# Expert routing set by VectorE's time, bfloat16 look-ups, and scattered weights laid out token by token

## The chip, the core and the metric

The kernel runs on one core of one Trainium2 chip. Five engines work side by side, each through a queue of its own in order: PE (TensorE, matrix products into PSUM), DVE (VectorE), ACT (ScalarE), POOL (GpSimd) and SP, which issues the loads. The metric is the device time in microseconds (us), the median of three runs: 2158.25 us (2157.36 to 2162.6).

## The reference

256 tokens of width 1024 pass through two blocks. What matters here is the PEER layer, which occurs twice in the second block. Its core:

```
q = (t @ w_q).reshape(n_tok, 8, 2, 128)                 # 8 heads, two halves
sc = einsum("thpd,hpnd->thpn", q, subkeys)              # 128 scores per half
sv, si = top_k(sc, 16)                                  # 16 best of each half
cand = sv[:, :, 0, :, None] + sv[:, :, 1, None, :]      # 256 sums per head
cidx = si[:, :, 0, :, None] * 128 + si[:, :, 1, None, :]
top_v, pos = top_k(cand, 16)
idx = take_along_axis(cidx, pos); g = softmax(top_v)    # 128 experts per token
h = einsum("cd,ced->ce", t, u_tab[idx])
a = g * gelu(h)
out = einsum("ce,ced->cd", a, v_tab[idx])
```

There are 16384 experts, each with a row of `u_tab` and of `v_tab`.

## The kernel before

The kernel gathers nothing. It multiplies all 256 tokens by all 128 tiles of `u_tab` (128 experts each; loop `for i in range(P)`, L1132), keeps the gelu of every product in `X` (`xa` for tiles below XA = 100, `xb` for the rest), and multiplies it by a weight that is zero for all experts that a token did not choose. Then `X` is multiplied by `v_tab` (L1178 onward).

**One step i of the loop.** `dense_t` (L136) fetches a 512 KB tile (one of four `raw` buffers), `split_now` (L109) makes it into a high part (`hi`, a cast on ACT, L121) and a low part (`lo`, a subtraction on DVE or POOL, L122), each with three buffers (HL), and PE runs 24 products of 256 columns into one of two PSUM banks (L132 to L134). ACT applies gelu (L1150, or L1146 followed by a product on DVE, L1147, once weights are there). For i below J1 + 2 = 42 the subtraction is on POOL, afterwards on DVE.

**Routing (i below J1 = 40).** It runs beside these steps, mostly on DVE, as a list of 36 jobs (L1118 to L1125) spread evenly by their count over the 40 steps. For each half `a` of the tokens: `candidates` and `best` find the 16 best of each head; `ranks` turns positions into two ranks; `weights` makes the softmax, with an Exp on ACT (L1064) between DVE's subtraction (L1062) and its sum (L1066); `keys` looks up the index behind each rank by comparing with 0 to 15 (L1050), multiplying with the list (L1055) and summing (L1057), in four calls of 64 ranks by 16 entries; `turn` transposes both keys and the weights on PE (L1078) and copies them, the keys with ACT (L1081), the weights with DVE (L1084). Two more functions, Exp and Gelu, each want a table on ACT, so each Exp between two gelus brings two table loads.

**Scatter (i from 40 to 123).** 64 times, for four tokens each, `scatter` compares both keys with 0 to 127 (`o`, L1092), multiplies by the weight in two parts (`wi`, L1099), and PE forms the four tokens' weights for all experts, eight products of 128 columns of float16 into one bank `G` (L1106). The bank is laid out token by token, each with 128 experts side by side. DVE multiplies the part for tiles already done into `X` (L1113), ACT copies the rest there (L1116); in `X` neighbouring experts of one token lie 1 KB apart.

**Order.** The Tile framework orders each engine's queue ahead of the run by the program order, its priorities and a modelled time. `split` has a priority 200 instructions ahead. `tc.issue_after(x)` puts those instructions of a block that run on x's engine behind x in that queue; it waits for nothing.

Of the kernel before, what the change touches and what calls it, by code (L numbers as in the profile page):

```python
# [10 lines left out]
F32 = mybir.dt.float32  # L11
F32R = mybir.dt.float32r
BF16 = mybir.dt.bfloat16
# [37 lines left out]
def two_blocks(ctx: ExitStack, tc: tile.TileContext, io, out):  # L51
# [37 lines left out]


    count, relief, fetched, pin, pinned = [0], [0], [0], [None], [0]

    more = []

# [14 lines left out]
    def split_now(raw, pool_share, into):  # L109
        count[0] += 1  # L110
        hi, lo = into or [stream.tile([P, D], F32R, tag=t, name=t, bufs=HL) for t in ("hi", "lo")]
        on_pool = pool_share and count[0] % pool_share == 0
        if relief[0] > 0 and into is None:
            relief[0] -= 1
            on_pool = True
        if pinned[0] > 0 and into is None:
            pinned[0] -= 1
            with tc.issue_after(pin[0]):
                S.copy(out=hi, in_=raw)
        else:  # L120
            S.copy(out=hi, in_=raw)  # L121
        (G if on_pool else V).tensor_tensor(out=lo, in0=raw, in1=hi.bitcast(F32), op=OP.subtract)  # L122
        return hi, lo

    def in_order(dst, src):
# [798 lines left out]
    def peer(l, entered, nxt):  # L924
        acts, nat = (xh, xl), entered.nat
        with ExitStack() as es:
            with ExitStack() as es1:
# [52 lines left out]
                for a in range(2):  # L980
# [4 lines left out]
                flat = X[1][:, 16:22].rearrange("p n g t -> p n (g t)")  # L985
# [3 lines left out]
                e = X[1][:, 20:22].rearrange("p n g t -> p (n g t)").bitcast(BF16).rearrange(  # L989
                    "p (n k) -> p n k", k=16)  # L990
                for n in range(12):
                    if n:
# [29 lines left out]
                def ranks(a):  # L1022
                    pos = state["pos"].rearrange("p h k -> p (h k)")
                    tmp = [one.tile([P, P], U32, tag=f"t{i}", name=f"t{i}") for i in range(4)]
                    V.tensor_scalar(tmp[0], pos, 4, None, op0=OP.logical_shift_right)
                    V.tensor_scalar(tmp[1], pos, 2, None, op0=OP.logical_shift_right)
                    V.tensor_scalar(tmp[2], pos, 15, None, op0=OP.bitwise_and)
                    V.tensor_scalar(tmp[3], pos, 3, None, op0=OP.bitwise_and)
                    m = one.tile([P, P], F32, tag="m_", name="m_")
                    V.tensor_scalar(m, pos, 64.0, None, op0=OP.is_ge)  # L1030
                    ra = one.tile([P, P], F32, tag="ra", name="ra")
                    rb = one.tile([P, P], F32, tag="rb", name="rb")
                    V.scalar_tensor_tensor(out=ra, in0=tmp[1], scalar=12.0, in1=tmp[0],
                                           op0=OP.subtract, op1=OP.subtract)
# [4 lines left out]
                    V.tensor_tensor(out=rb, in0=rb, in1=tmp[2], op=OP.add)  # L1039
                    state["rank"] = (ra, rb)  # L1040
# [5 lines left out]
                def keys(a, side, part):  # L1046

                    hs = slice(part * 4, part * 4 + 4)
                    cs = slice(part * 64, part * 64 + 64)
                    V.tensor_tensor(  # L1050
                        out=e, in0=state["rank"][side][:, cs].unsqueeze(2).to_broadcast([P, 64, 16]),
                        in1=iota_f[:, 0:16].unsqueeze(1).to_broadcast([P, 64, 16]), op=OP.is_equal)
                    lists = state["sif"].rearrange("q (h p) k -> q h p k", p=2)[:, hs, side]
                    e4 = e.rearrange("q (h k) a -> q h k a", h=4)
                    V.tensor_tensor(out=e4, in0=e4, in1=lists.unsqueeze(2).to_broadcast([P, 4, 16, 16]),  # L1055
                                    op=OP.mult)
                    V.tensor_reduce(out=state["key"][side][:, cs], in_=e, axis=AX.X, op=OP.add)  # L1057

                def weights(a):
                    tv = state["tv"]  # L1060
                    g = one.tile([P, 8, 16], F32, tag="g", name="g")
                    V.tensor_tensor(out=g, in0=tv, in1=tv[:, :, 0:1].to_broadcast([P, 8, 16]),  # L1062
                                    op=OP.subtract)
                    S.activation(out=g, in_=g, func=AF.Exp)  # L1064
# [6 lines left out]
                    state["g"] = g  # L1071

                def turn(a):
                    s = slice(a * P, (a + 1) * P)
# [12 lines left out]
                def scatter(tg, done):  # L1087
# [10 lines left out]
                    for i in range(2):  # L1098
# [1 line left out]
                            out=wi[i].rearrange("p n (b c) -> p n b c", c=4),  # L1100
                            in0=o[:, 0:4].rearrange("p n (b c) -> p n b c", c=4),
                            in1=gt[i][:, s].unsqueeze(2).to_broadcast([P, 4, 32, 4]), op=OP.mult)
                    ps = bank(p_tr, "G").rearrange("p (t i) -> p t i", t=4)
                    for t in range(4):
                        for i in range(2):
                            PE.matmul(out=ps[:, t], lhsT=o[:, 4 + t], rhs=wi[i][:, t],  # L1106
                                      start=i == 0, stop=i == 1)
                    for i0, xt in ((0, X[0]), (XA, X[1])):
                        n = xt.shape[1]
                        dst = xt[:, :, tg].rearrange("p i t -> p t i")  # L1110
                        old = min(max(done - i0, 0), n)
                        if old:
                            V.tensor_tensor(out=dst[:, :, :old], in0=ps[:, :, i0:i0 + old],  # L1113
                                            in1=dst[:, :, :old], op=OP.mult)
                        if old < n:
                            S.copy(out=dst[:, :, old:], in_=ps[:, :, i0 + old:i0 + n])  # L1116

                jobs = [lambda n=n: (subkeys(n), lists(n)) for n in range(12, 16)]  # L1118
                for a in range(2):
                    for part in range(2):  # L1120
                        jobs.append(lambda a=a, part=part: candidates(a, part))
                        jobs += [lambda a=a, h=h: best(a, h) for h in range(4 * part, 4 * part + 4)]
                    jobs.append(lambda a=a: (ranks(a), weights(a)))
                    jobs += [lambda a=a, s=s, p=p: keys(a, s, p) for s in range(2) for p in range(2)]
                    jobs.append(lambda a=a: turn(a))  # L1125
                at = {}
                for i, job in enumerate(jobs):
                    at.setdefault(i * J1 // len(jobs), []).append(job)
                for tg in range(64):
                    at.setdefault(J1 + tg * (J2 - J1) // 64, []).append(tg)  # L1130
                ready = 0
                for i in range(P):  # L1132
# [2 lines left out]
                        two = es1.enter_context(sbuf("gw2", 2, "right"))  # L1135
                    for job in at.get(i, []):
                        if callable(job):
                            job()
                        else:
                            scatter(job, i)  # L1140
                            ready = job + 1
                    ps = dense_t(io["peer_u"][l, i], acts, int(i < J1 + 2)).rearrange(
                        "p (g t) -> p g t", t=4)
                    if ready:
                        h = two.tile([P, 64, 4], F32, tag="h", name="h")
# [1 line left out]
                        V.tensor_tensor(out=xs(i)[:, :ready], in0=xs(i)[:, :ready], in1=h[:, :ready],  # L1147
                                        op=OP.mult)
                    if ready < 64:
                        S.activation(out=xs(i)[:, ready:], in_=ps[:, ready:], func=AF.Gelu)  # L1150
            acc = accumulators()
            late = []

# [194 lines left out]
```

## Time and profile before

| | |
|---|---|
| median of three runs | 2158.25 us |
| the profiled execution: time, span | 2159.3 us, 2157.5 us |
| PE busy | 2100.2 us (97%) |
| DVE busy | 1571.3 us (73%) |
| ACT busy | 1097.2 us (51%) |
| POOL busy | 348.9 us (16%) |
| mean granted TensorE clock | 0.988 of full speed |

The first PEER layer's steps i begin at about 443 us of the span and its scatter at about 568 us; the second layer's at about 1383 and 1507 us. In the rows further down, an idle time in brackets stands for the time before that instruction, with what ended it.

### The profile page before, as it was taken

What the parts mean: (1) busy time and instruction counts of PE and PEld (TensorE: products, weight loads), DVE (VectorE), ACT (ScalarE), POOL (GpSimd) and SP (SyncE); (2) the same over time, 40 slices, a digit from 0 to 9 for tenths busy, and PEclk for the clock granted to TensorE, in tenths of its full rate; (3) what the DMA queues carried; (4) which work ended last, traced back from release to release, by engine and by line L of the source; (5) the groups of instructions that cost most, each with busy time, mean ns of one, the idle gap of its engine ahead of it and who ended that gap; (6) DMA issues with size and microseconds to landing.
All of it is one profiled execution on the core that took longest, in us unless ns stands there. A gap on an engine that the chain in (4) does not pass through costs nothing. (4 is left out here: it accounts for less than half of the span.)

```text
span 2157.5 us, 37694 instructions
## 1 busy us (share of the span) xinstructions
PE 2100.2 (97%) x14288; PEld 1907.1 (88%) x14288; DVE 1571.3 (73%) x3045; ACT 1097.2 (51%) x1979; POOL 348.9 (16%) x167
## 2 busy tenths in 40 slices
PE   8999999998999999999999999989999999999998
PEld 7899989998999999888888777989999998888886
DVE  4456778699488998566566685995889996566565
ACT  4556545344555444555555574444554445555554
POOL 3210011278500000000000232588000000000000
PEclk9999999999999999999999999999999999999999
DMA  6634737345555455666666551545555456666664
GB/s 238 218 125 154 256 119 234 99 147 156 180 163 163 153 160 172 189 193 194 189 195 200 206 197 57 169 147 162 164 165 158 158 162 198 189 192 193 189 194 137
DMA packets 104437, 373.94 MB, mean 173 GB/s; under 512 B 12096, under 2 KB 14144, under 8 KB 103744
## 3 DMA queue, kind: packets, MB, share of 16 engines
q1 hardware_dynamic: 103968, 371.01, 54.8%
q8 instruction: 112, 1.84, 0.3%
q14 instruction: 69, 0.57, 0.1%
q10 hardware_dynamic: 288, 0.52, 0.1%
HBM read 370.44 MB, written 1.05 MB: 172 GB/s over the span
## 5 line engine op out<-in xcount | busy, mean ns | idle before, releaser
L132 PE MATMUL mm<-xh,hi 128*128 128x256 f32 x2880 | 834.9, 290 | 23.8 <-ACT xa L1150 22.2
L134 PE MATMUL mm<-xh,lo 128*128 128x256 f32 x2880 | 817.5, 284 | 0.4 <-POOL lo L122 0.4
L133 PE MATMUL mm<-xl,hi 128*128 128x256 f32 x2880 | 817.6, 284 | 0.0
L121 ACT CAST hi<-raw 128x1024 fp32r<-128x1024 f32 x600 | 632.5, 1054 | 283.6 <-issue 145.9
L122 DVE TENSOR_TENSOR lo<-raw,hi 128x1024 fp32r<-128x1024 f32 x484 | 592.2, 1223 | 248.1 <-ACT hi L121 244.0
L132 PEld LDWEIGHTS mm<-xh,hi 128*128 128x128 f32 x2880 | 555.1, 193 | 28.7 <-ACT xa L1150 23.7
L133 PEld LDWEIGHTS mm<-xl,hi 128*128 128x128 f32 x2880 | 555.6, 193 | 0.3
L134 PEld LDWEIGHTS mm<-xh,lo 128*128 128x128 f32 x2880 | 554.9, 193 | 1.0 <-POOL lo L122 0.8
L122 POOL TENSOR_TENSOR lo<-raw,hi 128x1024 fp32r<-128x1024 f32 x118 | 304.2, 2588 | 251.0 <-ACT hi L121 241.4
L1174 PE MATMUL acc<-hi,al 128*128 128x512 f32 x976 | 304.1, 393 | 0.0
L1174 PE MATMUL acc<-lo,ah 128*128 128x512 f32 x976 | 302.4, 391 | 0.0
L1174 PE MATMUL acc<-hi,ah 128*128 128x512 f32 x976 | 301.5, 390 | 0.0
L1174 PEld LDWEIGHTS acc<-hi,ah 128*128 128x128 f32 x976 | 183.1, 188 | 41.8
L1174 PEld LDWEIGHTS acc<-hi,al 128*128 128x128 f32 x976 | 183.4, 188 | 39.7
L1174 PEld LDWEIGHTS acc<-lo,ah 128*128 128x128 f32 x976 | 183.3, 188 | 38.7
L1163 ACT CAST ah<-xa 128x256 fp32r<-128x256 f32 x200 | 81.2, 407 | 241.5 <-PE acc L1174 241.5
L1164 DVE TENSOR_TENSOR al<-xa,ah 128x256 fp32r<-128x256 f32 x200 | 85.0, 426 | 99.2 <-PE acc L1174 99.2
L294 POOL TENSOR_TENSOR enl<-raw,enh 128x1024 fp32r<-128x1024 f32 x5 | 12.4, 2488 | 823.0 <-ACT enh L293 823.0
L1116 ACT COPY xa<-G 128x240 f32<-128x240 f32 (+22 forms) x92 | 35.1, 382 | 180.0 <-DVE xa L1113 139.0
L1113 DVE TENSOR_TENSOR xa<-G,xa 128x400 f32<-128x400 f32 (+31 forms) x128 | 111.4, 870 | 0.0
L1099 DVE TENSOR_TENSOR wi<-o,gt 128x512 f16<-128x512 f16 x256 | 106.5, 456 | 1.0
L1092 DVE TENSOR_TENSOR o<-iota_k,ij 128x1024 f16<-128x1024 f16 x128 | 94.6, 741 | 11.9 <-PE G L1106 10.7
(461 smaller groups left out, 2113.4 us busy)
## 6 DMA issues: line engine op xcount, KB each, us to landing
raw<-in_peer_u_dram SPq DMA_DIRECT2D x256, 512.0 KB, 3.6
raw<-in_peer_v_dram SPq DMA_DIRECT2D x256, 512.0 KB, 4.2
raw<-in_peer_w_q_dram SPq DMA_DIRECT2D x24, 512.0 KB, 3.8
raw<-in_conv_w_in_dram SPq DMA_DIRECT2D x20, 512.0 KB, 3.9
raw<-in_w_rest_dram SPq DMA_DIRECT2D x18, 512.0 KB, 3.8
raw<-in_w_qk_dram SPq DMA_DIRECT2D x16, 512.0 KB, 4.5
more<-in_w_rest_dram SPq DMA_DIRECT2D x10, 512.0 KB, 3.7
raw<-in_w_v_dram SPq DMA_DIRECT2D x8, 512.0 KB, 4.6
```

What stands on the lines that cost most here:

```text
L121: S.copy(out=hi, in_=raw)
L122: (G if on_pool else V).tensor_tensor(out=lo, in0=raw, in1=hi.bitcast(F32), op=OP.subtract)
L132: PE.matmul(out=ps, lhsT=ah, rhs=bh, start=first and i == 0, stop=False)
L133: PE.matmul(out=ps, lhsT=ah, rhs=bl, start=False, stop=False)
L134: PE.matmul(out=ps, lhsT=al, rhs=bh, start=False, stop=last and i == n - 1)
L1092: V.tensor_tensor(out=o.rearrange("p n (b c) -> p n b c", c=4), in0=iota_k.rearrange("p (b c) -> p b c", c=4).unsqueeze(1).to_broadcast(fo ...
L1099: V.tensor_tensor(out=wi[i].rearrange("p n (b c) -> p n b c", c=4), in0=o[:, 0:4].rearrange("p n (b c) -> p n b c", c=4), in1=gt[i][:, s]. ...
L1113: V.tensor_tensor(out=dst[:, :, :old], in0=ps[:, :, i0:i0 + old], in1=dst[:, :, :old], op=OP.mult)
L1116: S.copy(out=dst[:, :, old:], in_=ps[:, :, i0 + old:i0 + n])
L1163: S.copy(out=act[0], in_=src)
L1164: V.tensor_tensor(out=act[1], in0=src, in1=act[0].bitcast(F32), op=OP.subtract)
L1174: PE.matmul(out=acc[a][half], lhsT=p[:, s], rhs=r[:, half * 512:(half + 1) * 512], start=i == 0 and w == 0, stop=i == P - 1 and w == 2)
```

## The change

- **Jobs** carry a cost and a flag; they are placed by the sum of the costs (28 units) over JOBS = 35 steps instead of by count over 40. `weights` loses its first and second instruction to two jobs: `shifted` (the subtraction, together with `ranks`) and `exponentials` (the Exp, behind the last gelu in ACT's queue), which follow in the order `shifted` + `ranks`, two `keys`, `exponentials`, `weights`. `turn` comes TURN = 4 steps after `weights`.
- **Splits in the routing stage** are on POOL in steps of flagged jobs (lists, candidates, best), on DVE in steps of the others and from step 36 on.
- **Each job** is traced within `issue_after` the last split that ran on DVE.
- **Look-ups** take 128 ranks at once. The ranks are written four times over in bfloat16, the lists are bfloat16, and the sum is four additions of halves instead of a reduction. The two keys have two buffers each. The scratch `e` has twice the size.
- **`turn`** copies the keys with DVE.
- **`scatter`** lays the bank `G` out expert by expert with the four tokens side by side: PE's 128 output columns lie 16 bytes apart, and DVE and ACT read the bank straight and write runs of four tokens (16 bytes).

```
-J1, J2, LATE, XA = 40, 124, 6, 100
+JOBS, TURN, J1, J2, LATE, XA = 35, 4, 40, 124, 6, 100
...
+        low = (G if on_pool else V).tensor_tensor(out=lo, in0=raw, in1=hi.bitcast(F32),
+                                                  op=OP.subtract)
+        if not on_pool:
+            last_split[0] = low.ins
...
+                    rank = [one.tile([P, P, 4], BF16, tag=f"rank{i}", name=f"rank{i}")
+                            for i in range(2)]
...
-                    V.tensor_tensor(out=ra, in0=ra, in1=tmp[0], op=OP.add)
+                    V.tensor_tensor(out=rank[0], in0=four(ra), in1=four(tmp[0]), op=OP.add)
...
-                    state["key"] = [one.tile([P, P], F32, tag=f"key{i}", name=f"key{i}")
+                    state["key"] = [two.tile([P, P], F32, tag=f"key{i}", name=f"key{i}")
                                     for i in range(2)]
-                    state["sif"] = one.tile([P, 16, 16], F32, tag="sif", name="sif")
+                    state["sif"] = one.tile([P, 16, 16], BF16, tag="sif", name="sif")
...
+                def keys(a, side):
+
                     V.tensor_tensor(
+                        out=e.rearrange("q n (b c) -> q n b c", c=4),
+                        in0=state["rank"][side].unsqueeze(2).to_broadcast([P, P, 4, 4]),
+                        in1=iota_f[:, 0:16].rearrange("q (b c) -> q b c", c=4).unsqueeze(1)
+                        .to_broadcast([P, P, 4, 4]), op=OP.is_equal)
+                    lists = state["sif"].rearrange("q (h p) k -> q h p k", p=2)[:, :, side]
+                    e4 = e.rearrange("q (h k) a -> q h k a", h=8)
+                    V.tensor_tensor(out=e4, in0=e4, in1=lists.unsqueeze(2).to_broadcast([P, 8, 16, 16]),
                                     op=OP.mult)
-                    V.tensor_reduce(out=state["key"][side][:, cs], in_=e, axis=AX.X, op=OP.add)
+                    for n in (8, 4, 2):
+                        V.tensor_tensor(out=e[:, :, 0:n], in0=e[:, :, 0:n], in1=e[:, :, n:2 * n],
+                                        op=OP.add)
+                    V.tensor_tensor(out=state["key"][side], in0=e[:, :, 0], in1=e[:, :, 1], op=OP.add)
...
+                def exponentials():
+                    with tc.issue_after(state["gelu"]):
+                        S.activation(out=state["g"], in_=state["g"], func=AF.Exp)
...
-                        S.copy(out=ij[:, 32 * a:32 * a + 32, c],
+                        V.tensor_copy(out=ij[:, 32 * a:32 * a + 32, c],
...
-                    ps = bank(p_tr, "G").rearrange("p (t i) -> p t i", t=4)
+                    ps = bank(p_tr, "G").rearrange("p (t i) -> p i t", t=4)
...
-                            PE.matmul(out=ps[:, t], lhsT=o[:, 4 + t], rhs=wi[i][:, t],
+                            PE.matmul(out=ps[:, :, t], lhsT=o[:, 4 + t], rhs=wi[i][:, t],
...
-                            V.tensor_tensor(out=dst[:, :, :old], in0=ps[:, :, i0:i0 + old],
+                            V.tensor_tensor(out=dst[:, :old], in0=ps[:, i0:i0 + old],
...
+                jobs = [(1.1, True, lambda n=n: (subkeys(n), lists(n))) for n in range(12, 16)]
                 for a in range(2):
                     for part in range(2):
+                        jobs.append((0.3, True, lambda a=a, part=part: candidates(a, part)))
+                        jobs += [(0.5, True, lambda a=a, h=h: best(a, h))
+                                 for h in range(4 * part, 4 * part + 4)]
+                    jobs.append((2.0, False, lambda a=a: (shifted(a), ranks(a))))
+                    jobs += [(2.1, False, lambda a=a, s=s: keys(a, s)) for s in range(2)]
+                    jobs.append((0.2, False, exponentials))
+                    jobs.append((0.8, False, weights))
...
-                            job()
+                            with tc.issue_after(last_split[0]):
+                                job()
...
-                    ps = dense_t(io["peer_u"][l, i], acts, int(i < J1 + 2)).rearrange(
+                    ps = dense_t(io["peer_u"][l, i], acts, int(i < len(by_pool) and by_pool[i])).rearrange(
```

## Rows read from the trace of the kernel before

**Rows 1.** PE's timeline: start, duration, instruction, idle time before and its releaser.

```profile
468.30 0.58 PE L132 MATMUL mm<-xh,hi 128*128 128x256 f32 x1 [3.27 <-ACT xa L1150]
...
520.60 0.58 PE L132 MATMUL mm<-xh,hi 128*128 128x256 f32 x1 [5.65 <-ACT xa L1150]
...
1404.27 0.39 PE L132 MATMUL mm<-xh,hi 128*128 128x256 f32 x1 [3.27 <-ACT xa L1150]
...
1458.23 0.58 PE L132 MATMUL mm<-xh,hi 128*128 128x256 f32 x1 [9.20 <-ACT xa L1150]
```

**Rows 2.** ACT's timeline, three of the four Exps.

```profile
465.31 0.31 ACT L1064 ACTIVATE g<-g 128x128 f32<-128x128 f32 x1 [3.44 <-DVE g L1062]
...
517.61 0.31 ACT L1064 ACTIVATE g<-g 128x128 f32<-128x128 f32 x1 [5.18 <-DVE g L1062]
...
1455.23 0.31 ACT L1064 ACTIVATE g<-g 128x128 f32<-128x128 f32 x1 [8.74 <-DVE g L1062]
```

**Rows 3.** Windows: length, busy time by engine, PEclk, DMA share, GB/s.

```profile
474.00:476.00 2.00, 2.00 (x18) 2.00 (x17) 2.00 (x5) 0.99 (x2) 1.21 (x1) 0.89 0.66 246
...
524.00:526.00 2.00, 2.00 (x12) 2.00 (x12) 2.00 (x5) 0.10 (x1) 0.60 (x1) 0.59 0.36 57
...
1404.00:1406.00 2.00, 1.73 (x14) 1.73 (x15) 2.00 (x1) 1.44 (x3) 2.00 (x2) 1.00 0.00 0
...
1464.00:1466.00 2.00, 2.00 (x17) 2.00 (x17) 1.97 (x4) 0.91 (x2) 1.29 (x1) 0.93 0.51 197
```

**Rows 4.** Windows of the first layer: routing, early scatter, late scatter (PE, PEld, DVE, ACT, POOL).

```profile
460.00:545.00 85.00, 76.08 (x590) 75.53 (x590) 84.19 (x164) 38.99 (x58) 67.14 (x25) 0.92 0.49 150
580.00:740.00 160.00, 160.00 (x1477) 158.35 (x1476) 139.38 (x246) 84.11 (x224) 0.00 (x0) 1.00 0.52 162
740.00:840.00 100.00, 99.00 (x904) 96.96 (x903) 97.15 (x166) 43.66 (x119) 0.00 (x0) 1.00 0.51 159
```

**Rows 5.** DVE by form, 400 to 562 us: busy us, mean ns, idle before.

```profile
L1055 DVE TENSOR_TENSOR xb<-xb,sif 128x1024 bf16<-128x1024 bf16 x8 | 21.7, 2710 | 0.1
L1057 DVE TENSOR_REDUCE key<-xb 128x64 f32<-128x1024 bf16 x8 | 9.6, 1206 | 0.1
...
L1050 DVE TENSOR_TENSOR xb<-ra,iota_f 128x1024 bf16<-128x1024 f32 x4 | 8.3, 2083 | 0.0
L1050 DVE TENSOR_TENSOR xb<-rb,iota_f 128x1024 bf16<-128x1024 f32 x4 | 7.3, 1830 | 0.0
...
L1099 DVE TENSOR_TENSOR wi<-o,gt 128x512 f16<-128x512 f16 x2 | 5.2, 2626 | 0.0
L122 DVE TENSOR_TENSOR lo<-raw,hi 128x1024 fp32r<-128x1024 f32 x4 | 4.8, 1205 | 0.0
```

**Rows 6.** DVE by form, 560 to 845 us, where POOL is idle from 580 us.

```profile
L1099 DVE TENSOR_TENSOR wi<-o,gt 128x512 f16<-128x512 f16 x126 | 48.1, 423 | 0.5
L1092 DVE TENSOR_TENSOR o<-iota_k,ij 128x1024 f16<-128x1024 f16 x62 | 42.9, 691 | 6.0 <-PE G L1106 5.4
L1113 DVE TENSOR_TENSOR xa<-G,xa 128x400 f32<-128x400 f32 x18 | 19.7, 1092 | 0.0
...
L1147 DVE TENSOR_TENSOR xb<-xb,h 128x244 f32<-128x244 f32 x2 | 0.8, 424 | 0.0
...
L1113 DVE TENSOR_TENSOR xa<-G,xa 128x244 f32<-128x244 f32 x1 | 0.7, 710 | 0.0
```

**Rows 7.** DVE's timeline, its wait at the end of routing.

```profile
568.53 0.69 DVE L1084 CAST gt<-tr 128x512 f16<-128x512 f32 x1 [23.93 <-ACT ij L1081]
```

**Rows 8.** PE's timeline, one scatter's products and the step behind them.

```profile
1510.26 0.62 PE L1106 MATMUL G<-wi,o 128*128 128x128 f16 x8
1510.69 0.36 PE L132 MATMUL mm<-xh,hi 128*128 128x256 f32 x1
1510.89 0.28 PE L133 MATMUL mm<-xl,hi 128*128 128x256 f32 x1
1511.01 0.28 PE L134 MATMUL mm<-xh,lo 128*128 128x256 f32 x1
```

More of the change, by code (lines that the diff above doesn't have):

```diff
@@ L91, in two_blocks @@
     count, relief, fetched, pin, pinned = [0], [0], [0], [None], [0]
+    last_split = [None]
     more = []
@@ L1032, in ranks, with four @@
                     rb = one.tile([P, P], F32, tag="rb", name="rb")
+                    rank = [one.tile([P, P, 4], BF16, tag=f"rank{i}", name=f"rank{i}")
+                            for i in range(2)]
+                    def four(t):
+                        return t.unsqueeze(2).to_broadcast([P, P, 4])
                     V.scalar_tensor_tensor(out=ra, in0=tmp[1], scalar=12.0, in1=tmp[0],
@@ L1041, in ranks @@
-                    state["key"] = [one.tile([P, P], F32, tag=f"key{i}", name=f"key{i}")
+                    V.tensor_tensor(out=rank[1], in0=four(rb), in1=four(tmp[2]), op=OP.add)
+                    state["rank"] = rank
+                    state["key"] = [two.tile([P, P], F32, tag=f"key{i}", name=f"key{i}")
                                     for i in range(2)]
-                    state["sif"] = one.tile([P, 16, 16], F32, tag="sif", name="sif")
+                    state["sif"] = one.tile([P, 16, 16], BF16, tag="sif", name="sif")
@@ L1044, in ranks @@
                     V.tensor_copy(out=state["sif"], in_=si[a])
-                def keys(a, side, part):
-                    hs = slice(part * 4, part * 4 + 4)
-                    cs = slice(part * 64, part * 64 + 64)
+                def keys(a, side):
                     V.tensor_tensor(
[L1051 to L1055, printed above, removed]
-                                    op=OP.mult)
-                    V.tensor_reduce(out=state["key"][side][:, cs], in_=e, axis=AX.X, op=OP.add)
@@ L1062, in weights @@
-                    V.tensor_tensor(out=g, in0=tv, in1=tv[:, :, 0:1].to_broadcast([P, 8, 16]),
+                    state["g"] = one.tile([P, 8, 16], F32, tag="g", name="g")
+                    V.tensor_tensor(out=state["g"], in0=tv, in1=tv[:, :, 0:1].to_broadcast([P, 8, 16]),
                                     op=OP.subtract)
-                    S.activation(out=g, in_=g, func=AF.Exp)
+                def exponentials():
+                    with tc.issue_after(state["gelu"]):
+                        S.activation(out=state["g"], in_=state["g"], func=AF.Exp)
@@ L1065, in weights @@
+                def weights():
+                    g = state["g"]
                     z = one.tile([P, 8], F32, tag="gz", name="gz")
@@ L1115, in scatter @@
                         if old < n:
-                            S.copy(out=dst[:, :, old:], in_=ps[:, :, i0 + old:i0 + n])
-                jobs = [lambda n=n: (subkeys(n), lists(n)) for n in range(12, 16)]
+                            S.copy(out=dst[:, old:], in_=ps[:, i0 + old:i0 + n])
+                jobs = [(1.1, True, lambda n=n: (subkeys(n), lists(n))) for n in range(12, 16)]
                 for a in range(2):
                     for part in range(2):
[L1121 to L1125, printed above, removed]
@@ L1126, in peer @@
-                at = {}
-                for i, job in enumerate(jobs):
-                    at.setdefault(i * J1 // len(jobs), []).append(job)
+                        jobs.append((0.3, True, lambda a=a, part=part: candidates(a, part)))
[3 more added lines that the diff above has]
+                    jobs += [(2.1, False, lambda a=a, s=s: keys(a, s)) for s in range(2)]
@@ new lines, in peer @@
+                    jobs.append((0.2, False, exponentials))
+                    jobs.append((0.8, False, weights))
+                at, by_pool, spent, total = {}, [], 0, sum(n for n, _, _ in jobs)
+                for n, alone, job in jobs:
+                    i = int(spent * JOBS / total)
+                    spent += n
+                    at.setdefault(i, []).append(job)
+                    by_pool += [alone] * (int(spent * JOBS / total) - i)
+                    if job is weights:
+                        i += TURN
+                        at.setdefault(i, []).append(lambda a=int(i > J1 - 6): turn(a))
@@ L1129, in peer @@
+                by_pool = [True] + by_pool
                 for tg in range(64):
@@ L1149, in peer @@
                     if ready < 64:
-                        S.activation(out=xs(i)[:, ready:], in_=ps[:, ready:], func=AF.Gelu)
+                        state["gelu"] = S.activation(out=xs(i)[:, ready:], in_=ps[:, ready:],
+                                                     func=AF.Gelu).ins
             acc = accumulators()
```

15 lines of the change are left out of this document (5 added, 10 removed).

## The prediction

> **What bounds the kernel now.** I read the windows first. In the first 160 us of a scatter PE is busy for all 160.00 us, and in the last 100 for 99.00 [rows 4]: the expert layers run at PE's pace, and what other engines do there is hidden behind it. The exception is routing, where PE was busy for 76.08 of 85 us, at a mean granted clock of 0.92 [rows 4]. So next I asked PE's timeline for its idle times there: four, of 3.27, 5.65, 3.27 and 9.20 us, 21.4 us in both layers, each ended by ACT's gelu [rows 1]. ACT's timeline says why the gelu was late. Each time ACT stood before an Exp that waited for DVE's subtraction L1062: 3.44 us (twice, the row of one stands), 5.18 and 8.74 us [rows 2]. The order was fixed ahead, DVE was 84.19 of 85 us busy [rows 4] and behind it, and ACT, in order, held back the casts and gelus of the steps. PE's idle times are as long as ACT's waits to within 0.5 us, so the table loads around an Exp alone would cost PE next to nothing.
>
> The windows also show what followed a stall. After the first, PE restarted at 468.30 at the lower clock level (1.2 GHz, 0.50 of full), and the 2 us from 474 have 0.89, so the lower level ended 0.44 us into them, at 474.4: 6.1 us at half pace cost 3.1 us. In the same way 520.60 to 525.6 cost 2.5 us and 1458.23 to 1464.3 cost 3.0; after 1404.27 the clock was 1.00 [rows 1, 3]. That is 8.6 us more. **What stands to be won is 21.4 + 8.6 = 30.0 us**, and up to 2.0 us at the end of the two scatters (1.00 us idle in 100, the second layer taken as the first [rows 4]).
>
> **The Exp.** It becomes a job of its own. Its input is made in the job before `ranks`, and `exponentials` comes after 2.0 + 2 x 2.1 = 6.2 units of the costs. A unit is 35/28 = 1.25 steps; a step is 24 products at 0.12 us apart [rows 8], 2.88 us; so DVE has 6.2 x 3.6 = 22 us more than before, and it was never more than 8.74 us late [rows 2]. I take all four waits as gone: 30.0 us. The table loads stay. What could be late next is DVE's own result, below.
>
> **The look-ups.** Before, they cost DVE 21.7 + 9.6 + 8.3 + 7.3 = 46.9 us a layer [rows 5]. Much of this is waiting beside POOL: the same product L1099 of 512 float16 takes 2626 ns while POOL splits and 423 ns where POOL is idle [rows 5, 6]. The change keeps POOL off these steps. From 1024 elements in 691 ns and 512 in 423 [rows 6], a 16-bit operation costs 155 ns and 0.523 ns an element. One call of `keys`: 2048 twice (2 x 1.23), additions of 1024, 512, 256 and 128 (0.69, 0.42, 0.29, 0.22), 4.1 us; four calls 16.3 us. The ends: if the new patterns ran at half that rate (1.05 ns an element), 6016 elements and 6 x 0.155 us make 7.2 us a call, 29 us a layer; the end on the cheap side is 16.3 itself, since no row has a 16-bit product below 0.523 ns an element. I take 16.3: `o` (L1092) has the same runs of four.
>
> **The splits.** In exchange DVE takes them in steps of unflagged jobs: 2 x 7.2 of 28 units, 18 of 35 steps, at 1.21 us [rows 5], 21.7 us. The ranks, written four times, cost some 0.5 us more each, 2 us in all. DVE's routing work, some 100 us before (about 444 to 544 us at 84.19/85 [rows 4]), becomes 100 - 46.9 + 16.3 + 21.7 + 2 = 93 us, against 35 x 2.88 = 101 us and 4 steps (11.5 us) before `turn`. Before, DVE even waited 23.93 us for its last copy [rows 7], so the end of routing has room, and `turn` with two more copies on DVE (0.7 us each, as L1084 [rows 7]) costs PE nothing. The tie behind the last split is on DVE's queue alone and adds no wait: a job cannot get in front of the split of the step before it, which PE needs. It also cannot run far ahead, which DVE pays with idle time that nobody waits for. Two buffers for the keys take away a wait that would end in PE's queue; no row shows it, so nothing is counted.
>
> Where the cover is thin: in a look-up step DVE has 4.1 us of `keys` over 2.63 steps, 1.6 a step, plus 1.21 of split, 2.8 of 2.88. A split can be some 3.5 us late (three buffers: two steps, 5.76 us, less about 1.05 of cast and 1.21 of split). I count 2 us in both layers for low parts that come late: between 0 and the 22 us of a rival below.
>
> **The scatter.** Writing 4 bytes per 1 KB is what makes L1113 slow: from 244 to 400 elements it rises from 710 to 1092 ns, 2.45 ns an element, while L1147, with elements side by side, takes 424 ns for 244 [rows 6]. Runs of four would bring 400 elements to about 424 + 156 x 1.05 = 0.59 us, 0.5 us less in each scatter that is full. DVE's gain is hidden, since PE is the bound there; of the 2.0 us of idle time at the ends I take 1.5.
>
> Against it stands PE's own write: its 128 columns now lie 16 bytes apart in the bank. The eight products take 0.43 us (1510.26 to 1510.69 [rows 8]), 54 ns each, at the full clock. No row shows PE writing with a gap. The bounds: nothing, if the address of a column does not matter; or the price that the gap has for DVE, 2.45 against 1.05, which is 2.3 times: 0.43 x 1.3 x 128 scatters = 72 us. (Below nothing is excluded: 54 ns for 128 columns is 2.4 GHz, one column a cycle.) I take nothing, by the nearest row, the same instruction in the same memory [rows 8]; L1113 is another engine and writes to SBUF, 1 KB apart. It is the weakest step of this sum.
>
> The Trainium skill (PSUM — Partial Sum Buffer, Specifications) speaks against it: PSUM has lines of 8 bytes, and it says that "any non-contiguous AP slows matmuls significantly". It gives no factor. By it the sum would lose its sign; the rival below has the price, and no row here shows whether it holds.
>
> **The sum.** From the profiled execution's 2159.3 us: 21.4 idle + 8.6 clock + 1.5 end of scatter - 2 late splits = 29.5 us gained, 2129.8 us. That execution is 1.05 us above the median, so about **2129 us**.
>
> **Rivals.**
>
> 1. PE's spaced write is slow (the other side). Place: the eight products of each of 128 scatters, where PE has no idle time [rows 4], so all of it shows. If a product takes twice its 54 ns, 0.43 x 128 = 55 us are lost: 2129 + 55 = 2184 us; at 2.3 times 2201. It decides from 30/128 = 0.23 us a scatter, a product at 83 ns in place of 54. For: DVE's price for gaps. Against: it is the price of another memory at a wider gap. The page named above is for it.
>
> 2. DVE becomes the bound in routing. If the bfloat16 patterns run at half rate, a call takes 7.2 us, and with 2.63 splits (3.2 us) 10.4 us against 7.56: 2.8 us late a call, 11 us a layer, which neither the 3.5 us of slack nor PE can swallow. 22 us in both layers, and the fall of the clock after a stall [rows 3] some 3 us a layer: 2129 + 28 = 2157 us, no change. For: 2.8 of 2.88 us a step at the full rate. Against: L1092 with runs of four [rows 6]. At half of it: 2143.
>
> 3. The change does not do what it says: ACT is again put before a result that isn't there, since the order comes from modelled times. Half of the waits would leave 15 us: 2144; all of them 2158. Against: 22 us of room for at most 8.74 us.
>
> **How the numbers follow.** Forecast 0.56, with its own range of 2123 to 2141 (all late splits, or none and all of the idle time). Rival 1 0.29, mostly at 2184. Rival 2 0.10, half of it near 2157 and half at 2143. Rival 3 0.05, 2144 to 2158. What a measurement can tell from no change is 0.3%, 6.5 us: faster is below 2151.8. Faster: 0.56 + 0.05 + 0.03 = 0.64; same: 0.05 + 0.02, with 0.01 for a slight rival 1, 0.08; slower 0.28. With cases of both signs the range has to reach into rival 1: 2122 to 2186, which leaves out the upper part of rival 1 (about 0.1) and some below.
>
> **What would show it.** Right: no PE idle time above 1 us that gelu ends in the two routing stages, clock 1.00 there, ACT's Exp without a wait; `keys` at 1.2 us for 2048 elements; L1113 with 400 elements near 0.6 us; the eight products of G still 0.43 us from the first to the next step's product. Wrong: those eight products over 0.66 us (rival 1: then the time is above 2158); PE waiting for DVE's `lo` at L134 in look-up steps (rival 2); ACT waiting before an Exp (rival 3). The forecast falls as a whole if PE's idle time in routing is again some 20 us.

## The result: 2129.13 us, and the profile after

The changed kernel takes 2129.13 us (median of six runs, 2126.59 to 2130.5), the kernel before 2161.28 us in the same comparison: a ratio of 0.9849, 95% interval 0.9837 to 0.986. The forecast was 2129.0 us. The profiled execution took 2128.48 us, with a span of 2126.7 us and a mean granted clock of 0.992, where it was 0.988.

The page's costliest groups (out<-in, count | busy us, mean ns of one | idle before and its releaser) say that TensorE (PE) no longer waits for gelu; GpSimd (POOL) does 70 splits of the high and low parts (`lo`), where it did 118:

```profile
L136 PE MATMUL mm<-xh,hi 128*128 128x256 f32 x2880 | 830.4, 288 | 0.4 <-DVE k_l L636 0.4
L138 PE MATMUL mm<-xh,lo 128*128 128x256 f32 x2880 | 814.3, 283 | 0.4 <-DVE lo L123 0.4
```

Windows of the first layer's routing and of its scatter (length, busy time of PE, PEld, DVE, ACT, POOL, then PEclk, DMA share, GB/s), against [rows 4]:

```profile
441.00:580.00 139.00, 138.56 (x1172) 137.81 (x1171) 121.03 (x338) 70.71 (x112) 40.14 (x17) 1.00 0.59 178
580.00:740.00 160.00, 160.00 (x1478) 158.41 (x1477) 129.12 (x250) 82.07 (x223) 0.00 (x0) 1.00 0.54 163
740.00:842.00 102.00, 102.00 (x937) 101.05 (x936) 86.93 (x165) 49.00 (x119) 0.00 (x0) 1.00 0.52 161
```

But for 0.44 us of routing PE is busy throughout, at the higher clock level. ScalarE's (ACT's) timeline has the Exp without the wait of [rows 2], and both table loads are still there:

```profile
500.52 1.28 ACT L1079 ACT_TABLE_LOAD   x1
501.81 0.31 ACT L1079 ACTIVATE g<-g 128x128 f32<-128x128 f32 x1
503.12 1.28 ACT L1179 ACT_TABLE_LOAD   x1
```

VectorE (DVE) by form, 441 to 580 us, for the four new look-up calls of the first layer (answers to [rows 5]):

```profile
L1064 DVE TENSOR_TENSOR xb<-xb,sif 128x2048 bf16<-128x2048 bf16 x4 | 4.9, 1225 | 0.1
L1057 DVE TENSOR_TENSOR xb<-rank,iota_f 128x2048 bf16<-128x2048 bf16 x4 | 4.9, 1220 | 0.0
...
L1067 DVE TENSOR_TENSOR xb<-xb 128x1024 bf16<-128x1024 bf16 x4 | 2.7, 684 | 0.0
...
L1067 DVE TENSOR_TENSOR xb<-xb 128x512 bf16<-128x512 bf16 x4 | 1.7, 432 | 0.1
...
L1067 DVE TENSOR_TENSOR xb<-xb 128x256 bf16<-128x256 bf16 x4 | 1.6, 410 | 0.0
L1069 DVE TENSOR_TENSOR key<-xb 128x128 f32<-128x128 bf16 x4 | 1.6, 406 | 0.1
```

That is 17.4 us a layer. The multiplication of the scatter, DVE by form in 550 to 840 us, is down from 1092 ns [rows 6]:

```profile
L1130 DVE TENSOR_TENSOR xa<-G,xa 128x400 f32<-128x400 f32 x18 | 10.3, 570 | 5.5 <-PE G L1123 5.3
```

PE's timeline around one scatter: the eight spaced products take 1505.60 - 1505.17 = 0.43 us, as before [rows 8].

```profile
1505.17 0.62 PE L1123 MATMUL G<-wi,o 128*128 128x128 f16 x8
1505.60 0.36 PE L136 MATMUL mm<-xh,hi 128*128 128x256 f32 x1
```

**Where the time came from.** PE's timeline also gives marks. The score product `sc` opens the work before routing, the first product `G` the scatter, and the first `acc` the second expert pass. Those of after:

```profile
405.31 0.39 PE L969 MATMUL sc<-sk,xb 128*128 128x128 f32 x2
...
561.72 0.23 PE L1123 MATMUL G<-wi,o 128*128 128x128 f16 x1
...
846.87 0.62 PE L1204 MATMUL acc<-hi,ah 128*128 128x512 f32 x2
...
1326.83 0.39 PE L969 MATMUL sc<-sk,xb 128*128 128x128 f32 x2
...
1482.30 0.23 PE L1123 MATMUL G<-wi,o 128*128 128x128 f16 x1
...
1767.45 0.62 PE L1204 MATMUL acc<-hi,ah 128*128 128x512 f32 x2
```

Those of before (the second layer's `G`, at 1510.26, stands in [rows 8]):

```profile
402.77 0.39 PE L965 MATMUL sc<-sk,xb 128*128 128x128 f32 x2
...
572.17 0.62 PE L1106 MATMUL G<-wi,o 128*128 128x128 f16 x8
...
860.19 0.62 PE L1174 MATMUL acc<-hi,ah 128*128 128x512 f32 x2
...
1338.72 0.39 PE L965 MATMUL sc<-sk,xb 128*128 128x128 f32 x2
...
1798.26 0.62 PE L1174 MATMUL acc<-hi,ah 128*128 128x512 f32 x2
```

The mark `G` does not part the same work in both kernels: in after it stands three of the 256-column products later in PE's queue. Windows between the first two marks of before and of after, of the tile `mm` alone, count them (PE's count is the first in brackets; the second layer has the same counts):

```profile
402.77:572.17 169.40, 156.60 (x1224) 152.97 (x1224) 0.00 (x0) 19.17 (x51) 0.96 0.52 160
...
405.31:561.72 156.41, 152.08 (x1227) 148.52 (x1228) 0.00 (x0) 19.10 (x51) 1.00 0.58 174
```

Three products are 3 x 0.12 = 0.36 us a layer, which the second column takes over from the scatter to routing:

| stretch | gained by the marks, us | for the same work, us |
|---|---|---|
| routing (`sc` to `G`), layers 1 and 2 | 12.99 + 16.07 = 29.1 | 29.8 |
| scatter (`G` to `acc`), layers 1 and 2 | 2.87 + 2.85 = 5.7 | 5.0 |
| before the first layer's `sc`, and between the layers | -2.54 - 1.43 = -4.0 | -4.0 |
| second `acc` to the end | 0.0 | 0.0 |
| span | 30.8 | 30.8 |

### The profile page after: what moved, and what is told of

Same layout as the page of the kernel before. It is cut to its first block, busy times and chain, and to the rows that moved or that the text cites. A ratio compares the mean times of both kernels' runs of the same rounds, so it can differ in the third digit from the quotient of the medians.

```text
span 2126.7 us, 37692 instructions
## 1 busy us (share of the span) xinstructions
PE 2089.0 (98%) x14288; PEld 1899.0 (89%) x14288; DVE 1519.2 (71%) x3101; ACT 1095.3 (52%) x1971; POOL 216.4 (10%) x119
## 5 line engine op out<-in xcount | busy, mean ns | idle before, releaser
L123 DVE TENSOR_TENSOR lo<-raw,hi 128x1024 fp32r<-128x1024 f32 x532 | 650.6, 1223 | 260.2 <-ACT hi L122 256.9
L123 POOL TENSOR_TENSOR lo<-raw,hi 128x1024 fp32r<-128x1024 f32 x70 | 171.6, 2452 | 267.5 <-ACT hi L122 256.0
L1109 DVE TENSOR_TENSOR o<-iota_k,ij 128x1024 f16<-128x1024 f16 x128 | 88.2, 689 | 48.5 <-PE G L1123 48.2
L1133 ACT COPY xa<-G 128x240 f32<-128x240 f32 (+22 forms) x92 | 24.1, 262 | 148.2 <-DVE xa L1130 148.2
L1116 DVE TENSOR_TENSOR wi<-o,gt 128x512 f16<-128x512 f16 x256 | 96.5, 418 | 1.2
L1123 PE MATMUL G<-wi,o 128*128 128x128 f16 x1024 | 79.8, 220 | 0.0
```

Source lines behind the costliest of these rows:

```text
L123: low = (G if on_pool else V).tensor_tensor(out=lo, in0=raw, in1=hi.bitcast(F32), op=OP.subtract)
L1109: V.tensor_tensor(out=o.rearrange("p n (b c) -> p n b c", c=4), in0=iota_k.rearrange("p (b c) -> p b c", c=4).unsqueeze(1).to_broadcast(fo ...
L1116: V.tensor_tensor(out=wi[i].rearrange("p n (b c) -> p n b c", c=4), in0=o[:, 0:4].rearrange("p n (b c) -> p n b c", c=4), in1=gt[i][:, s]. ...
L1123: PE.matmul(out=ps[:, :, t], lhsT=o[:, 4 + t], rhs=wi[i][:, t], start=i == 0, stop=i == 1)
L1133: S.copy(out=dst[:, old:], in_=ps[:, i0 + old:i0 + n])
```

## The experiments

Medians in us. Each ratio is to the kernel before in the same comparison, where that took 2161.2 to 2162.6 us.

| run | what it is | us | ratio, 95% interval |
|---|---|---|---|
| e1 | before, Exp moved | 2170.74 | 1.0047, 1.003 to 1.0064 |
| e2 | after, Exp moved back | 2155.49 | 0.9972, 0.9961 to 0.9982 |
| e3 | after, old scatter layout | 2133.49 | 0.9876, 0.986 to 0.9893 |
| e4 | before, new scatter layout | 2156.73 | 0.9977, 0.9967 to 0.9988 |
| e5 | after, old look-ups | 2128.6 | 0.9852, 0.9835 to 0.9868 |
| e6 | after, routing's splits on POOL | 2187.42 | 1.0118, 1.0098 to 1.0137 |
| e7 | after, jobs not tied to the split | 2160.14 | 0.9995, 0.9983 to 1.0006 |
| e8 | after, one key buffer | 2128.45 | 0.9854, 0.9838 to 0.9871 |
| e9 | after, ordering parts alone | 2134.2 | 0.9868, 0.9852 to 0.9885 |
| e10 | after, jobs spread by count | 2130.44 | 0.9847, 0.983 to 0.9863 |
| e11 | after, Exp not tied to a gelu | 2153.37 | 0.996, 0.9944 to 0.9976 |
| e12 | e6, halves kept in order on DVE | 2159.44 | 0.9989, 0.9979 to 0.9999 |

**e1: the Exp's place alone.** In the kernel before, the Exp and the sum over it leave the job of the ranks for the later look-up jobs, and the subtraction stays there; the Exp is tied behind the last gelu, nothing else changes. The lines of the jobs:

```
...
-  jobs.append(lambda a=a: (ranks(a), weights(a)))
-  jobs += [lambda a=a, s=s, p=p: keys(a, s, p) for s in range(2) for p in range(2)]
+  jobs.append(lambda a=a: (shifted(a), ranks(a)))
+  jobs += [lambda a=a, p=p: keys(a, 0, p) for p in range(2)]
+  jobs.append(lambda a=a: (exponentials(), keys(a, 1, 0)))
+  jobs.append(lambda a=a: (keys(a, 1, 1), weights()))
...
```

> The kernel before, with one edit: the subtraction goes with the ranks, the Exp behind the last gelu at the third look-up call, the sum behind the fourth; number and places of the jobs, look-ups, splits and scatter as before. If the wait before the Exp is the cause, the four PE idle times (21.4 us) and the low clock behind them (8.6 us) go: 2161 - 30 = 2131 us, up to 2136 if the softmax now comes late for the transposes. If it takes a DVE with less work (short look-ups, no POOL beside them), the Exp or what comes after it still waits for a DVE that is behind: 2145 us or more.

Measured 2170.74 us: slower than before, so the theory that the Exp's wait is the whole matter fell, and the rival's 2145 us or more held. The waits for gelu are gone, but PE now stands at the transposes of `turn`: 2.78 us for a key, then 13.77 us for the weights `g`. PE's timeline in the first layer (the second has the same two, 2.78 and 13.78 us):

```profile
523.51 0.47 PE L1083 MATMUL tr<-ident,g 128*128 128x128 f32 x1 [13.77 <-DVE g L1075]
```

The Exp whose result PE misses had long been done; ACT's timeline:

```profile
500.24 0.31 ACT L1067 ACTIVATE g<-g 128x128 f32<-128x128 f32 x1
```

DVE's timeline shows what stood between: the sum over that Exp (`gz`, L1072) comes 22 us later in DVE's queue, behind the second half's ranks and first look-up.

```profile
518.12 0.23 DVE L1025 TENSOR_SCALAR t<-pos 128x128 uint32<-128x128 uint32 x1
...
520.01 1.21 DVE L1050 TENSOR_TENSOR xb<-ra,iota_f 128x1024 bf16<-128x1024 f32 x1
...
522.40 0.28 DVE L1072 TENSOR_REDUCE gz<-g 128x8 f32<-128x128 f32 x1
```

So the order of DVE's queue, set ahead, put the later half's work in front. That is the refined theory: each queue is in order, and wherever one holds an instruction ahead of its turn, PE pays.

**e2: the Exp back in the job of the ranks**, all else as after (it also loses its tie to a gelu).

```
...
-  jobs.append((2.0, False, lambda a=a: (shifted(a), ranks(a))))
+  jobs.append((2.0, False, lambda a=a: (ranks(a), shifted(a), exponentials(), softmax())))
...
```

> The kernel after, with the Exp and the rest of the softmax back in the job of the ranks, untied to the gelu; all else as after. ACT's queue then has the Exp behind 7 and 23 gelus of a layer instead of 19 and 33. If the wait before the Exp is the cause, ACT stands there again until DVE, which is tied to the steps, makes its input: some 5 us and 10 us a layer, 30 us in both with the clock behind them some 8 more: 2155 to 2170 us. If the lighter DVE is the cause, the input is there in time and the time stays at 2129 to 2133.

Measured 2155.49 us, as expected. Four waits for gelu are back, 17.6 us in all; PE's timeline has the first layer's second and longest:

```profile
529.46 0.58 PE L136 MATMUL mm<-xh,hi 128*128 128x256 f32 x1 [5.73 <-ACT xa L1181]
```

**e11: the Exp in its later job, but without the tie to the gelu.**

```
-  with tc.issue_after(state["gelu"]):
-      S.activation(out=state["g"], in_=state["g"], func=AF.Exp)
+  S.activation(out=state["g"], in_=state["g"], func=AF.Exp)
```

> The changed kernel without the Exp's tie behind the gelu; the Exp is issued from the same later job, but ScalarE's queue has it again behind 7 and 23 gelus in the two layers, as when it was put back into the ranks' job. Theory (what counts is where the Exp stands in ScalarE's queue): 2150 to 2157 us, TensorE waiting for gelu four times, 3 and 6 us. Rival (the tie to the split is enough, since it holds VectorE's shifted scores in place): 2127 to 2131 us, no such waits.

Measured 2153.37 us, and in PE's waits (us in total, times, longest) the same four as in e2:

```profile
PE mm L136 <- ACT xa L1178: 17.6, 4, 5.7
```

Each layer's two Exps have 7 and 23 gelus of the layer ahead of them in ACT's queue, as in e2; after has 19 and 33. The later job alone does not move the Exp; it takes the tie.

**e7: no tie behind the last split.**

```
-  with tc.issue_after(last_split[0]):
-      job()
+  job()
```

> The kernel after without the tie of each job behind DVE's last split. DVE's queue then has the ranks, a whole look-up and the next candidates ahead of the first split of that stretch. If the tie keeps splits in time, DVE comes to that split late by several us more than the 3.5 us of slack and PE waits for the low part: 2135 to 2160 us. If the tie only sets when DVE idles: 2127 to 2131.

Measured 2160.14 us: the whole gain is gone. PE's timeline in the first layer (the second: 5.02 and 7.23 us):

```profile
485.70 0.58 PE L138 MATMUL mm<-xh,lo 128*128 128x256 f32 x1 [5.02 <-DVE lo L123]
...
527.28 0.48 PE L1095 MATMUL tr<-ident,g 128*128 128x128 f32 x1 [7.19 <-DVE g L1087]
```

DVE's timeline holds both causes. The split that PE misses, at 484.44, stands behind candidates of the second half mixed into the first half's look-ups; and the sum `gz` of an Exp that ACT began at 510.82 and ended in 0.31 us stands at 522.48, behind the second half's first look-up.

```profile
479.10 0.35 DVE L1006 TENSOR_TENSOR cand<-xb 128x192 f32<-128x192 f32 x1
479.37 1.22 DVE L1064 TENSOR_TENSOR xb<-xb,sif 128x2048 bf16<-128x2048 bf16 x1
...
484.25 0.26 DVE L1020 MAX8 tv<-cand 128x8 f32<-128x112 f32 x1
484.44 1.20 DVE L123 TENSOR_TENSOR lo<-raw,hi 128x1024 fp32r<-128x1024 f32 x1
...
519.28 3.28 DVE L1057 TENSOR_TENSOR xb<-rank,iota_f 128x2048 bf16<-128x2048 bf16 x1
522.48 0.27 DVE L1084 TENSOR_REDUCE gz<-g 128x8 f32<-128x128 f32 x1
```

In the changed kernel the same sum runs at 505.82, 3.7 us after its Exp's end.

**e6: all splits of the routing stage on POOL.** With no split on DVE in that stage the tie has nothing to hold to, so it is lost too.

```
-  int(i < len(by_pool) and by_pool[i])
+  int(i < J1 + 2)
```

> The kernel after, with the splits of all steps below 42 on POOL, as before. Each 16-bit operation then stands beside POOL and takes 2 to 3 us instead of 0.4 to 1.2: some 60 us of look-ups a layer, DVE without splits 118 us of work against 112 us until the transposes. If the room counts: PE waits some 6 us a layer before the transposes, 2140 to 2150 us. If it does not: 2127 to 2131.

Measured 2187.42 us, worse than either theory had it. In each layer PE waits 5.1 us for a key at the first half's transposes, and then for the weights; PE's timeline:

```profile
540.27 0.47 PE L1095 MATMUL tr<-ident,g 128*128 128x128 f32 x1 [19.87 <-DVE g L1087]
```

The Exp ran at 505.67, its sum at 539.16, behind both look-ups of the second half. Two causes are mixed here, the order and POOL's company, so e12 takes the order out.

**e12: e6, with the second half's jobs behind the first half's softmax on DVE.** `state["w"]` is that softmax's last product.

```
-  with tc.issue_after(last_split[0]):
+  with tc.issue_after(state.get("w", last_split[0])):
```

> The kernel of e6 (all splits of the routing stage on GpSimd, 2187 us) with one order restored on VectorE: every job of the second half of the tokens stands behind the first half's last softmax product, so that its ranks and look-ups can't stand in front of the first half's sum. Nothing else is changed, and GpSimd still runs beside VectorE. Theory (e6 lost its time because the first half's sum stood behind the second half's work in VectorE's queue, and TensorE stood before the transpose, 19.9 us a layer): that wait goes or falls to a few us, 2129 to 2150 us, the upper end if the keys stay 5 us late as in e6. Rival (GpSimd beside VectorE costs the time by itself, VectorE being too slow in routing): 2165 to 2190 us, with TensorE waiting for the second half's transposes or for the weights in place of the first half's.

Measured 2159.44 us, between the two: the order was worth 28.0 us of e6's loss, as the theory said, and 30.3 us to the changed kernel are left, which the rival put down to POOL. The long wait is gone and four shorter ones are left in the first layer, of 3.76 and 0.64 us at the first half's transposes and of 6.13 and 0.49 us at the second's (the second layer has much the same; 21.9 us in all). PE's timeline has the longest:

```profile
567.79 0.48 PE L1095 MATMUL tr<-ident,key 128*128 128x128 f32 x1 [6.13 <-DVE key L1069]
```

No order of DVE's queue would take much of this away: from 460 us to the end of that wait at about 568.7, DVE is busy for 107.56 of 108.70 us, though it does none of the stage's splits. e12 differs from the changed kernel in its order too, so the 30.3 us are not POOL's alone by a single edit; that POOL's company is the cause rests on this busy time and on the look-ups. DVE by form, 441 to 580 us, has them: the look-ups take 61.5 us beside POOL, against 17.4 in the changed kernel.

```profile
L1057 DVE TENSOR_TENSOR xb<-rank,iota_f 128x2048 bf16<-128x2048 bf16 x4 | 13.5, 3384 | 0.1
L1064 DVE TENSOR_TENSOR xb<-xb,sif 128x2048 bf16<-128x2048 bf16 x4 | 13.2, 3312 | 0.1
L1067 DVE TENSOR_TENSOR xb<-xb 128x1024 bf16<-128x1024 bf16 x4 | 11.1, 2764 | 0.1
L1067 DVE TENSOR_TENSOR xb<-xb 128x512 bf16<-128x512 bf16 x4 | 8.0, 2003 | 0.1
L1067 DVE TENSOR_TENSOR xb<-xb 128x256 bf16<-128x256 bf16 x4 | 7.9, 1963 | 0.1
L1069 DVE TENSOR_TENSOR key<-xb 128x128 f32<-128x128 bf16 x4 | 7.8, 1952 | 0.1
```

**e5: the old look-ups in the changed kernel** (float32 ranks, two calls of 64 ranks a job, the reduction). Of its edit:

```
...
-  for n in (8, 4, 2):
-      V.tensor_tensor(out=e[:, :, 0:n], in0=e[:, :, 0:n], in1=e[:, :, n:2 * n], op=OP.add)
-  V.tensor_tensor(out=state["key"][side], in0=e[:, :, 0], in1=e[:, :, 1], op=OP.add)
+  V.tensor_reduce(out=state["key"][side][:, cs], in_=e, axis=AX.X, op=OP.add)
...
```

> The kernel after, with the look-ups of before (float32 ranks and lists, 64 ranks a call, a reduction), at the places of after and with POOL idle beside them. By the elements an operation of 1024 takes about 1.2 us without POOL, 3.6 us for 64 ranks, 29 us a layer against 16. If DVE's room is what I counted, a look-up step has 2.8 + 1.2 = 4.0 us of work in 2.88, 5.9 us late after both calls against 3.5 us of slack: PE waits some 2 to 3 us four times, with the clock 2139 to 2145 us. If DVE's work does not matter once the Exp waits for nobody: 2129 to 2131.

Measured 2128.6 us: the new look-ups are worth nothing that shows. DVE by form, 441 to 580 us, has the old ones at 29.3 us a layer without POOL, where they took 46.9 beside it [rows 5]:

```profile
L1059 DVE TENSOR_TENSOR xb<-xb,sif 128x1024 bf16<-128x1024 bf16 x8 | 9.8, 1225 | 0.3
...
L1061 DVE TENSOR_REDUCE key<-xb 128x64 f32<-128x1024 bf16 x8 | 9.7, 1213 | 0.0
...
L1054 DVE TENSOR_TENSOR xb<-rb,iota_f 128x1024 bf16<-128x1024 f32 x4 | 4.9, 1221 | 0.0
L1054 DVE TENSOR_TENSOR xb<-ra,iota_f 128x1024 bf16<-128x1024 f32 x4 | 4.9, 1216 | 0.0
```

Of the 29.5 us a layer by which they became shorter, 17.6 came from POOL's absence and 11.9 from the new form (bfloat16 ranks, additions of halves, half as many calls), and the 11.9 were not needed.

**e8: one buffer for the keys, copied by ACT.**

```
-  state["key"] = [two.tile([P, P], F32, ...
+  state["key"] = [one.tile([P, P], F32, ...
-  V.tensor_copy(out=ij[:
+  S.copy(out=ij[:
```

> The kernel after with one buffer for each key and the keys copied by ACT, both as before. I counted nothing for these two: 2127 to 2131 us. If the second buffer or DVE's copies matter: 2133 us or more.

Measured 2128.45 us: nothing, as counted.

**e3 and e4: the scatter's layout**, taken out of the changed kernel and put alone into the one before.

```
...
-  ps = bank(p_tr, "G").rearrange("p (t i) -> p i t", t=4)
+  ps = bank(p_tr, "G").rearrange("p (t i) -> p t i", t=4)
-  PE.matmul(out=ps[:, :, t], lhsT=o[:, 4 + t], rhs=wi[i][:, t], ...
+  PE.matmul(out=ps[:, t], lhsT=o[:, 4 + t], rhs=wi[i][:, t], ...
...
```

The lines shown are e3's edit; e4's is its reverse, in the kernel before.

> The kernel after, with the scatter's bank laid out token by token as before (PE's columns side by side, DVE and ACT writing 4 bytes per 1 KB). If PE's spaced write is free, only the 2 us of idle time at the ends of the scatters come back: 2131 us, the eight products 0.43 us in both. If PE's spaced write costs something that other gains hide, this kernel is faster than after: 2125 us or less.

> The kernel before, with the scatter's layout of after alone. If PE's spaced write is free: the 2 us at the ends of the scatters go, 2159 us, and the four waits before the Exps stay as they were. If the look of the scatter matters to the routing as well, 2150 us or less; if the spaced write costs, above 2163 us.

Measured 2133.49 us without the layout (+4.4) and 2156.73 us with it alone (-4.7): it is worth about 4.5 us in either kernel, more than expected. The traces put it where the change was made: for the same work, the stretch from `G` to `acc` is 2.5 us a layer longer in e3 than in the changed kernel, and 2.6 us shorter in e4 than in the kernel before. In e4 the four waits for gelu are all there, 21.4 us.

**e9: the ordering parts alone** (e3, e5 and e8 together).

> The changed kernel with everything put back that does not order the engines' queues: float32 look-ups, one key buffer with ScalarE's key copies, and the old layout of the scattered weights. Kept are the later place of the Exp, the tie to the last split, and the splits on VectorE. Theory (the three ordering parts together make the gain, the layout the remaining 4 to 5 us, the rest nothing): 2133 us (2130 to 2136), TensorE without a wait in the two routing stretches. Rival (look-ups and keys each hid only because the other was there; together they make VectorE or ScalarE late): 2140 to 2150 us, with TensorE waiting some us for lo or for the transposes.

Measured 2134.2 us. In 441 to 580 us PE is busy for 139.00 of 139. Place of the Exp, tie and splits together make the gain in routing, the layout the rest.

**e10: jobs spread by count, with the tie.**

```
+  jobs = [(1.0, alone, job) for _, alone, job in jobs]
```

> The changed kernel with every routing job given the same cost, so that the jobs are spread evenly by count over the steps instead of by VectorE's time; the tie stays. Theory (the tie alone keeps the queues in step, the spacing matters little): 2127 to 2131 us, no waits of TensorE over 1 us. Rival (the pacing by time is needed, since a step that takes several look-up calls overfills VectorE): 2134 to 2150 us, TensorE waiting for lo or for key.

Measured 2130.44 us, within what the runs can tell from 2129.13: the spacing by DVE's time is worth nothing that shows, as long as the jobs are tied. The edit also moves splits, since the flags follow the steps: POOL does 25 of them in 441 to 580 us, 17 in the changed kernel. PE is busy for 138.29 of the same 139 us.

## Why the prediction was right, and where it was not

**The waits for gelu and the clock: right in size.** The 21.4 us of idle time and 8.6 us of lower clock, less 2 us for late splits, made 28.0 us; the routing stretches gave 29.8 for the same work, with a clock of 1.00. The late splits cost 0.4 us in place of 2.

**The reason given for it was half of one.** The prediction said that the Exp "comes after 2.0 + 2 x 2.1 = 6.2 units of the costs", so "DVE has 6.2 x 3.6 = 22 us more". With the tie behind the gelu that room is there: in the changed kernel the first layer's two Exps begin 30.6 and 22.3 us after the end of their subtraction (L1074). e11 keeps the place in the list of jobs and takes away only the tie: its first Exp begins 0.03 us after its subtraction's end, and 24 us of the gain go. The queue's order was planned in modelled time, and the place in the program gave no room by itself. The 22 us were read as a property of the list; they were one of the list and `issue_after` together.

**The tie was taken as neutral and is essential.** "Adds no wait" was right. But it was priced only as something harmless, at nothing, while without it (e7) 31 us are lost. Rival 3, ACT put before a result that isn't there, had a chance of 0.05 because of the 22 us. Its mechanism is what e2 and e11 show as soon as the Exp loses its tie. e1, e6 and e7 show a relative of it on DVE that no rival named: the sum over the Exp, whose input has long been there, stands behind other work in DVE's queue. It was missed that moving the Exp later leaves DVE's sum over it free to stand anywhere in DVE's queue.

**POOL off the look-up steps: right, but not followed to the end.** The 46.9 us of look-ups were put down in good part to POOL's company. The old look-ups take 29.3 us without it (e5), and e12, with the new ones beside POOL, is 30.3 us slower than the changed kernel. The call was priced at 16.3 us a layer and takes 17.4; DVE's work of 93 us in 100 came out as 91.13 (444 to 544 us). Rival 2's half rate is excluded by 1220 ns for 2048 elements. What failed is the value of the new form of the look-ups, bfloat16 with it: e5 shows that DVE had room for the old look-ups too.

The Trainium skill bears on this in SBUF — State Buffer, Who interferes with whom: a VectorE instruction with two inputs in SBUF contends with a GpSimd instruction that reads SBUF, over a shared pair of ports that is locked and not divided. The rows agree with it: what POOL adds to one operation depends little on its size, 3384 - 1220 = 2.2 us for 2048 elements, 1963 - 410 = 1.6 us for 256, both less than one of e12's splits on POOL (2.66 us as a mean).

**The scatter: the term was mis-sized.** 1.5 us were counted and the stretches give 5.0 for the same work; e3 and e4 say 4.4 and 4.7. The term was read from the windows, where PE had 1.00 us of idle time in the last 100 us [rows 4]. That is where the gain lay, but the busy sum showed less than half of it, because the rows of products overlap. PE's timeline of before has one of these places:

```profile
751.68 0.62 PE L1106 MATMUL G<-wi,o 128*128 128x128 f16 x8
752.48 0.39 PE L132 MATMUL mm<-xh,hi 128*128 128x256 f32 x1 [0.18 <-ACT xa L1150]
```

The next product begins 0.80 us after the eight of `G` in place of 0.43, so PE lost 0.37 us, and the row of the product ahead covers half of that. Seven such places a layer, all between 739 and 836 us in the first, come to 2.2 us; the changed kernel and e4 have none. Up to the 40th scatter (739 us), where the windows had PE busy for 160.00 of 160, the new layout gained nothing: e4 comes to it as long after its first scatter as before does, 166.4 us. The gelu that PE waits for came late on ACT, which had stood shortly before it for DVE's multiplication of the scatter; ACT's timeline:

```profile
750.77 0.21 ACT L1116 COPY xa<-G 128x28 f32<-128x28 f32 x1 [2.18 <-DVE xa L1113]
```

How much of the gain is the multiplication (1092 ns before, 570 after, for 400 elements) and how much the copy itself (382 ns before, 262 after, as means) was not tried apart.

**PE's spaced write: right.** It was "the weakest step of this sum", with a chance of 0.29 for rival 1. The eight products take 0.43 us in both layouts, and the kernels with the spaced write (after, e4) are the faster ones. The Trainium skill's sentence in PSUM — Partial Sum Buffer, Specifications, that any non-contiguous pattern slows matmuls significantly, does not hold for these products; the measurement decides.

**The total is nearer than its parts, and that is luck.** 3.5 us more from the scatter and 1.8 more from routing met 4.0 us that were lost before the first layer and between the layers, which no step foresaw. Their cause stays open; over the profiled executions of all these kernels the first `sc` stood between 402.8 and 409.1 us, and the stretch between the layers took 475.2 to 480.5 us, so it may be no more than the spread of executions. Nor was the gain met to 0.1 us: 29.5 us were forecast, and the medians differ by 32.2, mostly because the kernel before took 2161.28 us in the comparison and 2158.25 when the forecast was made from it.

## What to carry to other kernels

Where each engine's order is fixed ahead by a model of time, look on every engine of a chain at what stands ahead of each link in its queue. Here the Exp on ACT and the jobs around it on DVE both needed their places given explicitly; ordering one of them only moved the wait (e1: slower than doing nothing; e7 and e11: 24 to 31 us of the gain gone). Before an operation is made cheaper, look whether a neighbour makes it dear: taking POOL away from the look-ups mattered, their cheaper form did not. And where an engine's rows overlap, a busy sum shows too little of a wait (1.0 us shown of some 2.2 us lost in a layer's scatter here): compare marks, with the same work between them.

## What the runs showed of the hardware

- A matmul that writes its 128 columns 16 bytes apart in its bank is as fast as one that writes them side by side: 0.43 us for eight, 54 ns each.
- The look-ups' 16-bit operations on DVE take beside POOL's splits 2.8 times as long at 2048 elements (3384 against 1220 ns) and 4.8 times at 256 and 128 (1963 against 410, 1952 against 406), as means of e12 and of the changed kernel.
- DVE's multiplication from PSUM into runs of four elements (16 bytes) takes 570 ns for 400 elements, into single elements 1 KB apart 1092 ns.
